# Ordering the next group's weight sums behind the running group's addition on VectorE, in a two-layer hybrid trunk

## The chip, the cores and the metric

The kernel runs on one core of a Trainium2 chip. The metric is the time of one execution on the device in microseconds (us). TensorE multiplies matrices, VectorE and ScalarE do elementwise work, GpSimd (POOL) does a little elementwise work and issues accumulating DMAs, and SyncE (SP) issues the loads. Each engine works through its own list of instructions in order; engines wait for each other on semaphores. Matrix products land in eight banks of PSUM, everything else lies in SBUF.

## The reference, cut to what matters

Two layers over 512 tokens of width 1024, all in float32. Each layer is a mixer with a residual and then a gated feed-forward part with a residual. The change touches only the feed-forward part:

```python
def gated_conv_ffn(x, w_gate, w_up, conv_w, conv_b, w_down):
    g = jnp.einsum('bsd,df->bsf', x, w_gate)        # 1024 -> 2816
    g = causal_dwconv3(g, conv_w) + conv_b          # width 3 along the tokens
    up = jnp.einsum('bsd,df->bsf', x, w_up)         # 1024 -> 2816
    return jnp.einsum('bsf,fd->bsd', jax.nn.silu(g) * up, w_down)

hn = rms_norm(h, norm_ffn[layer])
h = h + gated_conv_ffn(hn, w_ffn_gate[layer], w_ffn_up[layer], conv_ffn[layer],
                       b_conv_ffn[layer], w_ffn_down[layer])
```

The mixers (a short gated convolution and causal pooling in the first layer, chunked spatial gating in the second) and the final norm are not touched.

## The kernel before, in words

**Precision.** Every float32 operand is split into a high part `hi`, rounded to the matmul's input format, and the rest `lo = x - hi`. A product is three matmuls into one bank: hi by hi, hi by lo, lo by hi. ScalarE writes `hi` (names `whi_...`, `a_hi`), VectorE writes `lo` (`wlo_...`, `a_lo`). For some weights (`summed`, L116) ScalarE writes `-x` into `lo`, a DMA from GpSimd adds `x`'s raw value to it (L121), and ScalarE writes `hi` (L122).

**The groups of the feed-forward part.** The hidden width of 2816 is 22 tiles of 128 columns, taken two at a time; a group `f` is the tiles f and f+1. `PARTS` (L475) sets the order: groups 0, 2, then 4, then the pairs (6, 8), (10, 12), (14, 16) and (18, 20). After each entry of `PARTS` the tiles finished so far are multiplied with their rows of the down weight. So inside a pair the second group follows the first with no down product between. Groups from 4 on are computed by `both` (L636).

**One group in `both`.** The gate matrix ("g") and the up matrix ("u") of the group, 1024 rows by 256 columns each, and the tokens are seen as 2 by 2 blocks, and each matrix is multiplied in seven products instead of eight, by sums of blocks (a scheme of Strassen's kind). A product is 12 matmuls of 128 by 256. `ffn_weights` loads four raw tiles of 512 KB (gate and up, upper and lower half of the rows) into four buffers with the tag "raw"; the next group's loads take the same buffers. From the raw tiles come:

- L646-648: block a11 of both matrices, split by `halves` (`whi_a11` and `wlo_a11`, `whi_a` and `wlo_a` in the profile); it feeds product 1.
- L653, L654: VectorE sums `s12` (lower right blocks added, then one block taken off), split into `whi_s12` and `wlo_s12`; they feed products 5 and 6.
- L659, L660: VectorE differences `s34`, split likewise; they feed products 7 and 3.
- L661: the lower half of the raw rows, split by `summed`; it feeds products 2 and 4.

L694 multiplies in the order gate 1, up 1, gate 5, gate 6, up 5, up 6, gate 2, gate 7, up 2, up 7, gate 4, gate 3, up 4, up 3. Products 1, 6, 7 and 4 of a matrix add up in one bank ("a"), 5 and 3 in a second ("e"), and 2 has a third ("b"). After each product `after` (L680) takes out what is needed: ScalarE copies (L682) products 1, 6, 7 and the gate's 4 from bank "a" into `rows3` (gate, name `rows`) or `kept` (up) before the next product of that bank adds to it. VectorE adds product 2 (bank "b") and product 3 (bank "e") onto such a copy (L687). When product 7 has been copied, VectorE adds product 5 from bank "e" onto the copy (L692); only then may product 3 overwrite bank "e".

Behind the gate's products come the width-3 convolution (`conv`: ScalarE L505, VectorE twice L507 per tile), the SiLU on ScalarE (`s`, L513), the products with the up matrix (L703, L704, L707) and the split of the result (`act`: `a_hi` L247, `a_lo` L249).

**Who sets the order.** The instructions are recorded in the order of the program text, and a list scheduler orders each engine's list by priorities and by its own estimate of times, so that instructions of the next group can stand ahead of the running group's. Each engine then runs its list strictly in that order. `tc.keep_in_program_order` and `tc.add_manual_dep` can bind the order.

The lines that stand in question:

```python
nc.vector.tensor_tensor(s12[:, 0], r0[:, :, P:], r1[:, :, P:], ALU.add)          # L653
nc.vector.tensor_tensor(s34[:, 0], r0[:, :, :P], r0[:, :, P:], ALU.subtract)     # L659
nc.vector.tensor_tensor(d, pending[key, 5], d, ALU.add)                          # L692
```

Of the kernel before, what the change touches and what calls it, by code (L numbers as in the profile page):

```python
# [12 lines left out]
ALU = mybir.AluOpType  # L13
PSUM = bass.MemoryType.PSUM

P = 128
# [14 lines left out]
def tile_trunk(ctx: ExitStack, tc: tile.TileContext, x, norm_mix, norm_ffn, final_norm,  # L31
# [3 lines left out]
    nc = tc.nc  # L35
# [37 lines left out]
            ("bf", rows_of(b_conv_ffn[1]), NF)])  # L73

    inorder = tc.keep_in_program_order

    eps = small[:, 1:2]
    nc.gpsimd.memset(eps, EPS)
# [37 lines left out]
    def summed(raw, a, b, name):  # L116

        hi = wp.tile([P, a, b], F32R, tag="whi", bufs=6, name=f"whi_{name}")
        lo = wp.tile([P, a, b], F32R, tag="wlo", bufs=6, name=f"wlo_{name}")
        nc.scalar.activation(lo, raw, AF.Copy, scale=-1.0)  # L120
        nc.gpsimd.dma_start(lo, raw, accum_op=ALU.add)  # L121
        nc.scalar.activation(hi, raw, AF.Copy)  # L122
        return hi, lo
# [42 lines left out]
    class Norm:  # L166


        def __init__(self, name, gain, apart=False):
            self.name, self.gain, self.n, self.apart = name, gain, 0, apart  # L170
            self.ssq = tp.tile([P, S], F32, tag="ssq", bufs=1, name=f"ssq_{name}")
# [97 lines left out]
    def padded_tile():  # L269
        turn[0] += 1  # L270
        return padded[turn[0] % NPADDED]
# [209 lines left out]
    def ffn_weights(layer, f, order):  # L481
        cs = slice(f * P, (f + 2) * P)
        return {(key, half): fetch(
            (w_ffn_gate if key == "g" else w_ffn_up)[layer][half * 512 : (half + 1) * 512, cs]
            .rearrange("(k p) c -> p k c", p=P), 4, 256, f"{key}{layer}_{f}_{half}")
            for key, half in order}

    class Ffn:
# [8 lines left out]
        def __init__(self, layer, prm, norm, ap, sums):  # L497
            self.layer, self.prm, self.ap, self.acts = layer, prm, ap, {}
            self.norm, self.sums = norm, sums
            self.t23, self.t41 = {}, {}  # L500

        def conv(self, t, ft):
            ap, prm, n = self.ap, self.prm, f"{self.layer}_{ft}"
            c = ap.tile([P, S], F32, tag="c", bufs=2, name=f"c{n}")
            nc.scalar.activation(c, t[:, 0:S], AF.Copy, scale=prm("cf", ft))  # L505
            for i in (1, 2):
                nc.vector.scalar_tensor_tensor(c, t[:, i : S + i], prm("cf", i * NF + ft), c,  # L507
                                               op0=ALU.mult, op1=ALU.add)
            return c
# [126 lines left out]
        def both(self, f):  # L636

            layer, ap, n = self.layer, self.ap, f"{self.layer}_{f}"
            raws = ffn_weights(layer, f, [(key, half) for half in range(2) for key in "gu"])
            stat = {}  # L640

            def put(key, product, hi_lo, i):
                stat[key, product] = hi_lo[0][:, i], hi_lo[1][:, i]

            w = self.unit(f"a11_{n}")
            for i, key in enumerate("gu"):  # L646
                self.halves(w[0][:, i], w[1][:, i], raws[key, 0][0][:, :, :P])
                put(key, 1, w, i)
            for key in "gu":
                r0, r1 = raws[key, 0][0], raws[key, 1][0]  # L650
                s12, s34 = (ap.tile([P, 2, 4, P], F32, tag="sum", bufs=3, name=f"{x}{key}_{n}")
                            for x in ("s12", "s34"))
                nc.vector.tensor_tensor(s12[:, 0], r0[:, :, P:], r1[:, :, P:], ALU.add)  # L653
                nc.vector.tensor_tensor(s12[:, 1], s12[:, 0], r0[:, :, :P], ALU.subtract)  # L654
                w = self.unit(f"s12{key}_{n}")
                self.halves(*w, s12)
                put(key, 5, w, 0)
                put(key, 6, w, 1)
                nc.vector.tensor_tensor(s34[:, 0], r0[:, :, :P], r0[:, :, P:], ALU.subtract)  # L659
                nc.vector.tensor_tensor(s34[:, 1], r1[:, :, :P], s12[:, 1], ALU.subtract)  # L660
                hi, lo = summed(*raws[key, 1])  # L661
                for i, product in enumerate((2, 4)):
                    c = slice(i * P, (i + 1) * P)
                    stat[key, product] = hi[:, :, c], lo[:, :, c]
                w = self.unit(f"s34{key}_{n}")
                self.halves(*w, s34)
                put(key, 7, w, 0)
                put(key, 3, w, 1)

            banks = {"g": {}, "u": {}}  # L670
            kept = ap.tile([P, 3, HALF], F32, tag="kept", bufs=1, name=f"kept{n}")
            pads = [padded_tile() for _ in range(2)]
            lo, hi = slice(2, 2 + HALF), slice(2 + HALF, 2 + S)
            dst = {("g", 1): pads[0][:, lo], ("g", 6): pads[0][:, hi], ("g", 7): pads[1][:, hi],
                   ("g", 4): pads[1][:, lo]}
            dst.update({("u", product): kept[:, i, :] for i, product in enumerate((1, 6, 7))})
            onto = {2: 1, 5: 7, 3: 6}
            s, pending = {}, {}

            def after(key, product, ps):  # L680
                if (key, product) in dst:
                    nc.scalar.copy(dst[key, product], ps)  # L682
                elif product == 5 and (key, 7) not in pending:
                    pending[key, 5] = ps
                elif product in onto:
                    d = dst[key, onto[product]]
                    nc.vector.tensor_tensor(d, ps, d, ALU.add)  # L687
                if (key, product) == ("u", 4):
                    pending["u", 4] = ps
                if product == 7:  # L690
                    d = dst[key, 7]
                    nc.vector.tensor_tensor(d, pending[key, 5], d, ALU.add)  # L692

            for key, product in (("g", 1), ("u", 1), ("g", 5), ("g", 6), ("u", 5), ("u", 6),  # L694
                                 ("g", 2), ("g", 7), ("u", 2), ("u", 7), ("g", 4), ("g", 3),
                                 ("u", 4), ("u", 3)):
                after(key, product, self.multiply(banks[key], f"{key}{n}", product,
                                                  stat[key, product]))
                if (key, product) == ("g", 4):
                    s[1] = self.silu(self.conv(pads[1], f + 1), f + 1)  # L700
                elif (key, product) == ("g", 3):
                    s[0] = self.silu(self.conv(pads[0], f), f)
            nc.vector.tensor_tensor(s[1][:, HALF:], kept[:, 2, :], s[1][:, HALF:], ALU.mult)  # L703
            nc.vector.tensor_tensor(s[1][:, :HALF], pending["u", 4], s[1][:, :HALF], ALU.mult)  # L704
            self.act(f + 1, s[1])
            s0 = s[0].rearrange("p (a b) -> p a b", a=2)
            nc.vector.tensor_tensor(s0, kept[:, :2, :], s0, ALU.mult)  # L707
            self.act(f, s[0])
# [284 lines left out]
```

## Time and profile before

| | |
|---|---|
| three runs | 1005.27, 1007.35, 1007.23 us; median 1007.23 |
| profiled execution | 1007.18 us, its span 1005.5 us |
| granted TensorE clock | 0.996 |
| TensorE busy | 988.0 us, 98% of the span, 5835 matmuls |
| VectorE busy | 699.3 us, 70%, 1057 instructions |
| ScalarE busy | 521.9 us, 52% |
| GpSimd busy | 100.8 us, 10% |
| HBM read, written | 98.42 MB, 2.10 MB |

How to read it: the profile is of one execution. A row of the timeline has a start and a duration in us, the engine, the line of the kernel, the operation, the tile written and the tiles read with buffer numbers left out, the shape, and in square brackets how long the engine was idle just before, with the engine, tile and line that released it. Rows that follow each other alike are merged (x4). Tile names carry the group: `g_6e` is bank "e" of the gate matrix in group 6; whether a row belongs to layer 0 or 1 is told by its time: the feed-forward part of layer 0 ends before 500 us and that of layer 1 begins after 620 us. `s12g`, `s34u` and the like carry the matrix, and `whi`/`wlo` in front of them are their high and low parts. A time is in the clock of the span.

### The profile page before, as it was taken

What the parts mean: (1) busy time and instruction counts of PE and PEld (TensorE: products, weight loads), DVE (VectorE), ACT (ScalarE), POOL (GpSimd) and SP (SyncE); (2) the same over time, 40 slices, a digit from 0 to 9 for tenths busy, and PEclk for the clock granted to TensorE, in tenths of its full rate; (3) what the DMA queues carried; (4) which work ended last, traced back from release to release, by engine and by line L of the source; (5) the groups of instructions that cost most, each with busy time, mean ns of one, the idle gap of its engine ahead of it and who ended that gap; (6) DMA issues with size and microseconds to landing.
All of it is one profiled execution on the core that took longest, in us unless ns stands there. A gap on an engine that the chain in (4) does not pass through costs nothing.

```text
span 1005.5 us, 14738 instructions
## 1 busy us (share of the span) xinstructions
PE 988.0 (98%) x5835; PEld 875.6 (87%) x5835; DVE 699.3 (70%) x1057; ACT 521.9 (52%) x775; POOL 100.8 (10%) x117
## 2 busy tenths in 40 slices
PE   8999999999999999999999999999999999999997
PEld 6788888898999989899888888888999899898895
DVE  5877457968776786867933545399667867687577
ACT  5622345744653746537655443675446366363563
POOL 2132020300000000000300001211000010000100
PEclk9999999999999999999999999999999999999999
DMA  6522224454454545545433222445446465454532
GB/s 222 191 96 92 85 84 126 105 150 123 129 147 129 162 113 132 147 115 167 134 118 105 74 93 91 98 97 132 129 105 156 117 142 152 102 152 125 123 109 83
DMA packets 81905, 124.53 MB, mean 124 GB/s; under 512 B 4293, under 2 KB 53677, under 8 KB 81837
## 3 DMA queue, kind: packets, MB, share of 16 engines
q1 hardware_dynamic: 73580, 98.96, 31.1%
q0 software_dynamic: 6912, 23.07, 12.5%
q10 hardware_dynamic: 1344, 1.58, 0.5%
q8 instruction: 45, 0.74, 0.3%
q14 instruction: 24, 0.19, 0.1%
HBM read 98.42 MB, written 2.10 MB: 100 GB/s over the span
## 4 chain that ended last, share of the span: by engine, by line
PE 81%; issue 7%; DMA 5%; DVE 5%; ACT 2%; POOL 0%; SPq 0%; ACTq 0%; DVEq 0%; POOLq 0%
PE gu L133 3%; PE gu L134 3%; PE gu L135 3%; PE d L133 3%; PE d L134 3%; PE d L135 3%; PE dn L133 2%; PE dn L135 2%; PE dn L134 2%; DMA raw_g<-in_w_ffn_gate_dram 2%; PE u L135 1%; PE oo L135 1%; PE u L134 1%; PE oo L133 1%; PE u L133 1%
## 5 line engine op out<-in xcount | busy, mean ns | idle before, releaser
L507 DVE SCALAR_TENSOR_TENSOR c<-rows,prm,c 128x512 f32<-128x512 f32 x88 | 67.7, 792 | 4.4 <-ACT c L505 4.1
L134 PE MATMUL d<-a_lo,whi_d 128*128 128x512 f32 x176 | 68.6, 390 | 0.0
L133 PE MATMUL dn<-whi_dn,a_hi 128*128 128x512 f32 x176 | 68.6, 390 | 0.0
L134 PE MATMUL dn<-wlo_dn,a_hi 128*128 128x512 f32 x176 | 68.6, 390 | 0.0
L135 PE MATMUL d<-a_hi,wlo_d 128*128 128x512 f32 x176 | 68.5, 389 | 0.0
L135 PE MATMUL dn<-whi_dn,a_lo 128*128 128x512 f32 x176 | 67.3, 390 | 0.0
L133 PE MATMUL d<-a_hi,whi_d 128*128 128x512 f32 x176 | 66.9, 390 | 0.0
L121 POOL DMA_DIRECT2D wlo_g<-raw_g x22 | 19.1, 868 | 382.1 <-ACT wlo_g L120 315.9
L922 DVE TENSOR_TENSOR y<-dn,y 128x512 f32<-128x512 f32 x48 | 32.3, 686 | 22.8 <-PE dn L135 22.3
L120 ACT ACTIVATE wlo_g<-raw_g 128x1024 fp32r<-128x1024 f32 x22 | 23.2, 1055 | 42.4 <-PE dn L134 42.4
L129 DVE TENSOR_TENSOR wlo_u<-raw_u,whi_u 128x1024 fp32r<-128x1024 f32 x16 | 19.6, 1224 | 34.2 <-ACT whi_u L128 34.1
L513 ACT ACTIVATE s<-c,prm 128x512 f32<-128x512 f32 x44 | 30.8, 716 | 21.5 <-DVE c L507 21.5
L633 ACT ACTIVATE whi_s12u<-s12u 128x1024 fp32r<-128x1024 f32 x18 | 18.9, 1049 | 43.2 <-PE d L134 33.8
L633 ACT ACTIVATE whi_s12g<-s12g 128x1024 fp32r<-128x1024 f32 x18 | 19.1, 1061 | 41.7 <-DVE s12g L654 36.1
L129 DVE TENSOR_TENSOR wlo_dn<-raw_dn,whi_dn 128x1024 fp32r<-128x1024 f32 x22 | 26.8, 1221 | 19.0 <-ACT whi_dn L128 19.0
L135 PEld LDWEIGHTS dn<-whi_dn,a_lo 128*128 128x128 f32 x176 | 33.0, 188 | 7.5 <-DVE a_lo L249 0.2
L134 PEld LDWEIGHTS d<-a_lo,whi_d 128*128 128x128 f32 x176 | 33.0, 188 | 7.3 <-DVE a_lo L249 0.2
L133 PEld LDWEIGHTS dn<-whi_dn,a_hi 128*128 128x128 f32 x176 | 33.0, 188 | 7.1 <-ACT a_hi L247 0.2
L129 DVE TENSOR_TENSOR wlo_d<-raw_d,whi_d 128x1024 fp32r<-128x1024 f32 x22 | 26.8, 1221 | 17.9 <-ACT whi_d L128 17.9
L133 PEld LDWEIGHTS d<-a_hi,whi_d 128*128 128x128 f32 x176 | 32.8, 188 | 7.1
L292 DVE TENSOR_TENSOR h<-d,h 128x512 f32<-128x512 f32 x48 | 32.5, 685 | 9.3 <-PE d L135 9.3
L135 PEld LDWEIGHTS d<-a_hi,wlo_d 128*128 128x128 f32 x176 | 33.0, 188 | 6.8
(1201 smaller groups left out, 3423.4 us busy)
## 6 DMA issues: line engine op xcount, KB each, us to landing
raw_g<-in_w_ffn_gate_dram SPq DMA_DIRECT2D x36, 512.0 KB, 4.1
raw_u<-in_w_ffn_up_dram SPq DMA_DIRECT2D x36, 512.0 KB, 4.5
wlo_g<-raw_g POOLq DMA_DIRECT2D x22, 512.0 KB, 4.6
raw_d<-in_w_ffn_down_dram SPq DMA_DIRECT2D x22, 512.0 KB, 3.6
raw_dn<-in_w_ffn_down_dram SPq DMA_DIRECT2D x22, 512.0 KB, 3.5
wlo_u<-raw_u POOLq DMA_DIRECT2D x18, 512.0 KB, 4.6
raw_oe<-in_w_out_even_dram SPq DMA_DIRECT2D x8, 512.0 KB, 3.6
raw_g<-in_w_ffn_gate_dram SPq DMA_DIRECT2D x16, 256.0 KB, 2.8
```

What stands on the lines that cost most here:

```text
L120: nc.scalar.activation(lo, raw, AF.Copy, scale=-1.0)
L121: nc.gpsimd.dma_start(lo, raw, accum_op=ALU.add)
L129: nc.vector.tensor_tensor(lo, raw, hi.bitcast(F32), ALU.subtract)
L133: nc.tensor.matmul(ps, lhs[0], rhs[0], start=start, stop=False)
L134: nc.tensor.matmul(ps, lhs[0], rhs[1], start=False, stop=False)
L135: nc.tensor.matmul(ps, lhs[1], rhs[0], start=False, stop=stop)
L292: nc.vector.tensor_tensor(h[k], ps, h[k], ALU.add)
L507: nc.vector.scalar_tensor_tensor(c, t[:, i : S + i], prm("cf", i * NF + ft), c, op0=ALU.mult, op1=ALU.add)
L513: nc.scalar.activation(s, c, AF.Silu, bias=self.prm("bf", ft))
L633: nc.scalar.activation(hi, src, AF.Copy)
L922: nc.vector.tensor_tensor(dst, ps, dst, ALU.add)
```

## The change: an order between two instructions of VectorE

`Ffn` remembers, for each of the two matrices, the last recorded addition L692. In the next group, the first sum of `s12` (L653) and the first difference of `s34` (L659) of the same matrix get a dependency on it that is only an order on the same engine, with no semaphore. Nothing is computed otherwise, and no buffer changes. In the first group of `both` there is no earlier addition, and no dependency. The dependency also holds where a down product lies between two groups.

```diff
+    def behind(ins, first):
+
+        if first is not None:
+            tc.add_manual_dep(ins.ins, first.ins.name, mybir.DependencyInfo(
+                mybir.DependencyClass.NoSync, mybir.DependencyReason.DATA), reason="order")
...
             self.t23, self.t41 = {}, {}
+            self.added = {"g": None, "u": None}
...
-                nc.vector.tensor_tensor(s12[:, 0], r0[:, :, P:], r1[:, :, P:], ALU.add)
+                behind(nc.vector.tensor_tensor(s12[:, 0], r0[:, :, P:], r1[:, :, P:], ALU.add),
+                       self.added[key])
                 nc.vector.tensor_tensor(s12[:, 1], s12[:, 0], r0[:, :, :P], ALU.subtract)
...
-                nc.vector.tensor_tensor(s34[:, 0], r0[:, :, :P], r0[:, :, P:], ALU.subtract)
+                behind(nc.vector.tensor_tensor(s34[:, 0], r0[:, :, :P], r0[:, :, P:],
+                                               ALU.subtract), self.added[key])
                 nc.vector.tensor_tensor(s34[:, 1], r1[:, :, :P], s12[:, 1], ALU.subtract)
...
                 if product == 7:
                     d = dst[key, 7]
-                    nc.vector.tensor_tensor(d, pending[key, 5], d, ALU.add)
+                    self.added[key] = nc.vector.tensor_tensor(d, pending[key, 5], d, ALU.add)
```

In the changed kernel every line from `behind` on has a number that is 6 to 9 higher: L692 is L701 there.

## The prediction

> **What bounds the kernel now.** I read the page first, then the waits of TensorE in its timeline, and from each of them back along VectorE and ScalarE. From the page:
>
> ```profile
> span 1005.5 us, 14738 instructions
> ...
> PE 81%; issue 7%; DMA 5%; DVE 5%; ACT 2%; POOL 0%; SPq 0%; ACTq 0%; DVEq 0%; POOLq 0%
> ```
>
> TensorE carries the chain, so only what makes TensorE wait can be won. Its timeline, a start and a duration in us per row, has these waits in the stage that the change touches:
>
> ```profile
> 451.47 0.39 PE L624 MATMUL g_18e<-hgh,whi_s34g 128*128 128x256 f32 x1 [0.59 <-DVE rows L692]
> ...
> 759.91 0.38 PE L624 MATMUL g_6e<-hgh,whi_s34g 128*128 128x256 f32 x1 [1.07 <-DVE rows L692]
> 760.13 0.28 PE L624 MATMUL g_6e<-hgl,whi_s34g 128*128 128x256 f32 x1
> 760.25 0.28 PE L624 MATMUL g_6e<-hgh,wlo_s34g 128*128 128x256 f32 x1
> ...
> 820.61 0.50 PE L624 MATMUL u_10a<-t,whi_s34u 128*128 128x256 f32 x2 [1.02 <-ACT kept L682]
> ...
> 823.99 0.38 PE L624 MATMUL g_10e<-hgh,whi_s34g 128*128 128x256 f32 x1 [0.25 <-DVE rows L692]
> ...
> 951.41 0.39 PE L624 MATMUL g_18e<-hgh,whi_s34g 128*128 128x256 f32 x1 [2.44 <-DVE rows L692]
> ```
>
> Four of the five are the first matmul of the gate's product 3 (the bank "e" of the running group), held by the addition L692 on VectorE, which must read product 5 out of that bank first. The fifth, 820.61, is the up matrix's product 7, held by ScalarE's copy L682 of product 6. Each costs more than its idle figure: a record of 0.28 stands for a step of 0.12 (760.13 to 760.25), so 0.16 of the wait lies under the record before, and the step behind the wait is 0.22 (759.91 to 760.13), 0.10 too long. So delay = idle + 0.26: 0.85, 1.33, 1.28, 0.51, 2.70, in all 6.67 us. The VectorE rows ahead of two of them show why:
>
> ```profile
> 758.23 0.69 DVE L653 TENSOR_TENSOR s12u<-raw_u,raw_u 128x512 f32<-128x512 f32 x1 [1.66 <-DMA raw_u<-in_w_ffn_up_dram]
> 758.84 0.68 DVE L659 TENSOR_TENSOR s34u<-raw_u 128x512 f32<-128x512 f32 x1
> 759.44 0.41 DVE L692 TENSOR_TENSOR rows<-g_6e,rows 128x256 f32<-128x256 f32 x1
> ...
> 949.19 0.69 DVE L653 TENSOR_TENSOR s12u<-raw_u,raw_u 128x512 f32<-128x512 f32 x1 [4.20 <-DMA raw_u<-in_w_ffn_up_dram]
> 949.80 1.22 DVE L634 TENSOR_TENSOR wlo_s12g<-s12g,whi_s12g 128x1024 fp32r<-128x1024 f32 x1
> 950.93 0.42 DVE L692 TENSOR_TENSOR rows<-g_18e,rows 128x256 f32<-128x256 f32 x1
> ```
>
> At 758.23 VectorE had sat 1.66 us, at 949.19 it had sat 4.20 us, waiting for the load of the next group's up weights (L653), with L692 of the running group queued behind. L692 starts 1.21 and 1.74 us after the landing and TensorE 0.06 us after its end (759.85 to 759.91). ScalarE has the same queueing at 820.61 (and the running group's copy of product 7 at 882.26 in a quiet case):
>
> ```profile
> 819.24 1.06 ACT L633 ACTIVATE whi_s12g<-s12g 128x1024 fp32r<-128x1024 f32 x1 [4.86 <-DVE s12g L654]
> 820.20 0.35 ACT L682 COPY kept<-u_10a 128x256 f32<-128x256 f32 x1
> ...
> 882.26 0.37 ACT L682 COPY rows<-g_14a 128x256 f32<-128x256 f32 x1 [0.39 <-PE g_14a L624]
> ```
>
> The copy `kept` at 820.20 needed only TensorE, but stood behind `whi_s12g`, which had waited 4.86 us for the next group's sums.
>
> **The change part by part.** No instruction is added or removed, and no semaphore: the order is between instructions of one engine. Set against each other, the two programs differ at eight places, the four handovers 6 to 8, 10 to 12, 14 to 16 and 18 to 20 of each layer. There L687 and L692 of the gate now stand ahead of the next group's gate sums, and both gate and up additions ahead of its up sums. The scheduler follows up elsewhere: ScalarE's `kept` copies move ahead of `whi_s12g`; s34u's last sum (L660) with its `whi` and `wlo` goes behind `wlo_s12u`; `wlo_s34g` and the two `a_lo` go ahead of `wlo_s12u`; TensorE takes the up product 5's second part 10 matmuls later, behind the gate's product 6.
>
> *What goes.* L692 now waits only for the copy of product 7, which ends at 882.63 in the handover 14 to 16, 3.8 us before product 3 starts there:
>
> ```profile
> 886.40 0.38 PE L624 MATMUL g_14e<-hgh,whi_s34g 128*128 128x256 f32 x1
> ```
>
> So the four L692 waits end; and the one on `kept` too, because that copy no longer has `whi_s12g` ahead of it. That is 6.67 us, plus the 0.10 that the row at 886.40 lost to a wait of 0.02: 6.77 us.
>
> *What comes.* Eight additions and sums now run later, so I walk VectorE's new order through 14 to 16. Steps between starts come from rows: 0.60 for 128x512 (758.84 to 759.44), and from these
>
> ```profile
> 888.13 0.42 DVE L687 TENSOR_TENSOR rows<-g_14e,rows 128x256 f32<-128x256 f32 x1
> 889.38 2.74 DVE L507 SCALAR_TENSOR_TENSOR c<-rows,prm,c 128x512 f32<-128x512 f32 x4 [0.82 <-ACT c L505]
> 892.04 0.42 DVE L687 TENSOR_TENSOR kept<-u_14e,kept 128x256 f32<-128x256 f32 x1
> 892.37 1.22 DVE L634 TENSOR_TENSOR wlo_s34g<-s34g,whi_s34g 128x1024 fp32r<-128x1024 f32 x1
> 893.50 0.42 DVE L703 TENSOR_TENSOR s<-kept,s 128x256 f32<-128x256 f32 x1
> ```
>
> 0.33 for 128x256 (892.04 to 892.37), 1.13 for 128x1024 (892.37 to 893.50), 0.66 for one L507 (four from 889.38 to 892.04). Product 3 now ends 0.12 earlier, so L687 starts at 888.01. Behind it two up sums: 888.34, 888.94. The four L507 run from 889.54 instead of 889.38, `kept` 892.20, L703 892.53, L704, L707 893.19, `wlo_s34g` 893.79, two `a_lo` 894.92 and 895.52, `wlo_s12u` 896.12 to 897.34. ScalarE beside it:
>
> ```profile
> 891.76 1.32 ACT L513 ACTIVATE s<-c,prm 128x512 f32<-128x512 f32 x2
> 892.99 1.04 ACT L122 ACTIVATE whi_u<-raw_u 128x1024 fp32r<-128x1024 f32 x1
> 893.93 1.04 ACT L633 ACTIVATE whi_s34u<-s34u 128x1024 fp32r<-128x1024 f32 x1
> 894.88 1.14 ACT L247 ACTIVATE a_hi<-s 128x512 fp32r<-128x512 f32 x2
> 895.92 1.05 ACT L120 ACTIVATE wlo_u<-raw_u 128x1024 fp32r<-128x1024 f32 x1
> 896.87 0.35 ACT L682 COPY rows<-g_16a 128x256 f32<-128x256 f32 x1
> ...
> 898.93 1.06 ACT L128 ACTIVATE whi_dn<-raw_dn 128x1024 fp32r<-128x1024 f32 x1 [1.44 <-PE g_16a L624]
> ```
>
> L703 needs `s`, whose first half ends about 892.5: in time. With `whi_s34u` gone from 893.93 the two `a_hi` take 893.93 to 894.97, and the copy `rows` of the next gate product 1 runs 894.97 to 895.32.
> TensorE, from 886.38 in steps of 1.44 per product: the next group's product 1 of gate 890.70 and up 892.14, gate 5 at 893.58; then, in the new order, 2 matmuls of up 5 and 1 of gate 2; gate 6 at 895.38; 2 of up 6 and 4 of gate 2; the rest of up 5 at 897.54. Gate 6 needs `rows`: 895.32 + 0.06 = 895.38, nothing to spare. The rest of up 5 needs `wlo_s12u`: 897.34 + 0.06 = 897.40, 0.14 to spare. A wait of any size costs the 0.10 behind it, so I take 0.10 for each of the seven handovers like this one, 0.70 us; the ends are 0 (`rows` just in time, as 886.40 nearly was) and 0.30 (`rows` 0.20 late).
>
> *Late loads.* Up sums now stand behind L692 of up, about 0.95 us after product 4 starts, so a landing up to then costs nothing. In 6 to 8 of layer 1 product 3 was due at 759.91 - 1.23 = 758.68, product 4 at 757.24, the sum could start at 758.2, the load was in at 758.23. In 18 to 20 of layer 1 product 3 was due at 951.41 - 2.60 = 948.81, its load was in at 949.19, 0.87 past that point. There the walk from 949.19 is: `wlo_s12g` 949.80, L687 950.93, three up sums, L507 from 953.06, `kept` 955.72, L703, L704, `wlo_s34g` 956.71, L707, one `a_lo`, `wlo_s12u` 959.04 to 960.26. TensorE's order there puts all of gate 2 ahead of the rest of up 5, due at 959.37. So 0.95 + 0.10 = 1.05 us of the 2.70 stays. It goes to 0 if the load lands 0.9 earlier, which can be: the load of `fin` (512 KB, ScalarE's queue) now is issued behind `whi_s12g` rather than beside this load. In the other handovers the sum followed straight on other work or came early; I take their loads as in time.
>
> *What is covered.* L660 of s34u, its `whi` and `wlo` end about 900.3; the product that reads them comes at 903.8. The first down-weight load must wait for the later gate sums, until about 885.3; the page gives its flight:
>
> ```profile
> raw_dn<-in_w_ffn_down_dram SPq DMA_DIRECT2D x22, 512.0 KB, 3.5
> ```
>
> so it lands near 889, and its reader `whi_dn` starts at 898.93. If this cover of 10 us went, each handover would pay the rest. The later loads of SP's queue wait for POOL's accumulating DMAs, as before. `wlo_u` goes out about 0.3 earlier; POOL's order is the same.
>
> *Sum.* Against the profiled execution's 1007.18 us (the median of the runs shown is 1007.23, so nothing is corrected): 1007.18 - 6.77 + 1.05 + 0.70 = 1002.2 us.
>
> **The rivals.**
> 1. All waits go: `rows` is in time everywhere and the load lands early. 1007.18 - 6.77 = 1000.4. For it: 886.40 waited 0.02 only. Against it: nothing to spare seven times over.
> 2. The tight place gives more: 0.35 in each of seven handovers, where ScalarE or VectorE runs 0.25 late. 1007.18 - 6.77 + 1.05 + 2.45 = 1003.9.
> 3. The stall moves: VectorE or `rows` comes some 0.7 late at each of eight places, and what L692 gave is paid at gate 6 and up 5 again; about 1007. The rows speak against it: ScalarE's chain from 888 to 893 stays as it was, since `s` is set by ScalarE's own order.
> 4. Slower: VectorE starts an instruction only when the one before has ended. Then the walk goes by durations, not by steps: from 888.01 0.42, 2 x 0.68, 4 x 0.75, 3 x 0.42, 0.68, 1.22, 2 x 0.68, 1.22 make 898.53, 1.05 past its point, with the 0.10 behind it 1.15 at seven places and 1.05 + 0.85 in 18 to 20: 1007.18 - 6.77 + 8.05 + 1.90 = 1010.4. It decides from 0.7 us per handover on. Against it: 758.84 starts 0.08 before the end of 758.23's record, and all rows above step so. The Trainium skill's page VectorE: DVE Perf Modes (The DRAIN you can't avoid) states that the next op does not start until the pipe has emptied after the one before. By that rule the time is this rival's; the trace disagrees with it in 0.61 steps under 0.69 records.
> 5. The change does nothing: excluded, the order of eight handovers changes.
>
> **How the numbers follow.** The forecast 0.60; rival 1 0.12; rival 2 0.12; rival 3 0.08; rival 4 0.08. A measurement of this kernel tells about 0.2%, 2 us, from no change. Faster by more: the first three, 0.84; same 0.08; slower 0.08. The range leaves out rivals 3 and 4: from 1000.2, just under rival 1, to 1005.0, rival 2 with the runs' own scatter (1005.27 to 1007.35 before).
>
> **What would show it.** In the changed profile product 3 (g_6e, g_10e, g_14e, g_18e) waits for no L692 (there L701), u_10a not for `kept`; L653 of the next group starts behind L692. Right at the tight place: short waits of g_8a, g_12a, g_16a and g_20a for `rows`, or of u_8e and its like for `wlo_s12u`; a wait of about 1 us at u_20e of layer 1. The prediction is wrong if these exceed 0.4 us each, or if loads of up weights land over 1 us later than here.

## The result, and the profile after

| | before | after |
|---|---|---|
| median | 1007.13 us (6 runs, 1004.08 to 1007.48) | 1000.98 us (6 runs, 1000.02 to 1002.09) |
| profiled execution | 1007.18 us | 1000.02 us |
| TensorE, VectorE, ScalarE busy | 988.0, 699.3, 521.9 us | 986.5, 699.9, 522.7 us |

The ratio is 0.9948, with a 95% interval of 0.9933 to 0.9962: 5.2 us less (3.8 to 6.7); the medians differ by 6.2. The forecast was 1002.2 us in a range of 1000.2 to 1005.0, faster with 0.84. The page of the changed kernel:

```profile
span 998.3 us, 14727 instructions
...
PE 92%; DVE 4%; DMA 2%; ACT 1%; issue 0%; SPq 0%; POOL 0%; DVEq 0%; ACTq 0%; POOLq 0%
```

The engines do the same work: TensorE, VectorE, ScalarE and GpSimd have 5835, 1057, 775 and 117 instructions in both pages, and the busy times move by 1.5 us at most, so what was won is waiting. The shares of the chain that ends last do not measure it: TensorE has 92% where it had 81%, and "issue" fell from 7% to 0%, which is some 70 us, where 5 us were won. Without the waits the chain takes another way back through the program; e9 below, still faster than before, has TensorE at 77%. TensorE's timeline of the changed kernel, at the places that the prediction named:

```profile
765.20 0.28 PE L631 MATMUL g_8b<-hgh,whi_g 128*128 128x256 f32 x1
765.32 0.51 PE L631 MATMUL g_8a<-t,whi_s12g 128*128 128x256 f32 x2
765.66 0.29 PE L631 MATMUL g_8a<-t,wlo_s12g 128*128 128x256 f32 x1
...
881.12 0.28 PE L631 MATMUL g_14e<-hgh,whi_s34g 128*128 128x256 f32 x1
...
954.59 0.39 PE L631 MATMUL u_20e<-t,wlo_s12u 128*128 128x256 f32 x1 [0.33 <-DVE wlo_s12u L641]
```

Product 3 of the gate (`g_14e`, 881.12) has no bracket, and neither have `g_6e`, `g_10e`, `g_18e` and `u_10a`: the five waits are gone in both layers. One wait is new, 0.33 idle at `u_20e`. At 765.32 two matmuls run before 765.66: 0.34 for two steps of 0.12, so one step was 0.10 too long, at the place where `rows` was to have nothing to spare. The same long step stands at `g_8a`, `g_12a`, `g_16a` and `g_20a` of both layers, eight in all. VectorE in the handover 18 to 20 of layer 1:

```profile
939.83 0.42 DVE L701 TENSOR_TENSOR rows<-g_18e,rows 128x256 f32<-128x256 f32 x1 [1.42 <-ACT rows L691]
940.17 0.68 DVE L660 TENSOR_TENSOR s12g<-raw_g,raw_g 128x512 f32<-128x512 f32 x1
940.77 0.69 DVE L667 TENSOR_TENSOR s34g<-raw_g 128x512 f32<-128x512 f32 x1
...
943.03 0.42 DVE L701 TENSOR_TENSOR kept<-u_18e,kept 128x256 f32<-128x256 f32 x1
943.37 0.68 DVE L660 TENSOR_TENSOR s12u<-raw_u,raw_u 128x512 f32<-128x512 f32 x1
...
952.72 0.68 DVE L255 TENSOR_TENSOR a_lo<-s,a_hi 128x512 fp32r<-128x512 f32 x1
953.32 1.22 DVE L641 TENSOR_TENSOR wlo_s12u<-s12u,whi_s12u 128x1024 fp32r<-128x1024 f32 x1
```

The addition (L701, L692 before) now comes first and has waited only for the copy of product 7; the first up sum at 943.37 follows the up addition with no idle time, where before it had held VectorE for 4.20 us.

Not all of the 7.2 us between the two profiled spans is the change. To tell it apart I measure from the start of each feed-forward part's first matmul to the start of its last: from the first `gu` to the last `d` in layer 0, the second `gu` to the program's last matmul in layer 1. The rows of before and, behind them, of after:

```profile
149.51 0.39 PE L133 MATMUL gu<-hgh,whi_g 128*128 128x512 f32 x1
...
497.79 0.39 PE L135 MATMUL d<-a_hi,wlo_d 128*128 128x512 f32 x1
...
640.79 0.48 PE L133 MATMUL gu<-hgh,whi_g 128*128 128x512 f32 x1
...
997.65 0.39 PE L135 MATMUL dn<-whi_dn,a_lo 128*128 128x512 f32 x1
```

```profile
147.92 0.39 PE L139 MATMUL gu<-hgh,whi_g 128*128 128x512 f32 x1
...
495.43 0.39 PE L141 MATMUL d<-a_hi,wlo_d 128*128 128x512 f32 x1
...
638.44 0.48 PE L139 MATMUL gu<-hgh,whi_g 128*128 128x512 f32 x1
...
990.52 0.39 PE L141 MATMUL dn<-whi_dn,a_lo 128*128 128x512 f32 x1
```

Layer 0 takes 348.28 before and 347.51 after, layer 1 takes 356.86 and 352.08: 0.77 + 4.78 = 5.55 us won in the two parts. The other 1.59 us were already there at the first `gu` (149.51 to 147.92), in work that the change doesn't touch. "Stage gain" below is this sum against before's 705.14 us; it needs no median, and a second profile of the changed kernel (e11) gives 5.43. Before's stage is from one profile; e3, which leaves layer 0 as it was, has 348.61 there where before has 348.28, so differences of 0.3 us say little.

### The profile page after: what moved, and what is told of

It is laid out like the page before. It is cut to its first block, busy times and chain, and to the rows that moved or that the text cites. A ratio compares the mean times of both kernels' runs of the same rounds, so it can differ in the third digit from the quotient of the medians.

```text
span 998.3 us, 14727 instructions
## 1 busy us (share of the span) xinstructions
PE 986.5 (99%) x5835; PEld 874.5 (88%) x5835; DVE 699.9 (70%) x1057; ACT 522.7 (52%) x775; POOL 100.6 (10%) x117
## 3 DMA queue, kind: packets, MB, share of 16 engines
q10 hardware_dynamic: 1344, 1.58, 0.5%
## 4 chain that ended last, share of the span: by engine, by line
PE 92%; DVE 4%; DMA 2%; ACT 1%; issue 0%; SPq 0%; POOL 0%; DVEq 0%; ACTq 0%; POOLq 0%
PE d L139 4%; PE d L140 4%; PE d L141 4%; PE dn L139 4%; PE dn L140 3%; PE dn L141 3%; PE gu L139 3%; PE gu L141 3%; PE gu L140 3%; PE u L141 1%; PE oo L141 1%; PE oo L139 1%; PE u L140 1%; PE u L139 1%; PE oe L140 1%; PE oe L139 1%
## 5 line engine op out<-in xcount | busy, mean ns | idle before, releaser
L641 DVE TENSOR_TENSOR wlo_s34u<-s34u,whi_s34u 128x1024 fp32r<-128x1024 f32 x18 | 22.1, 1226 | 26.1 <-ACT whi_s34u L640 26.1
L140 PEld LDWEIGHTS dn<-wlo_dn,a_hi 128*128 128x128 f32 x176 | 33.1, 188 | 6.5
```

The lines of the kernel that those rows point to most:

```text
L140: nc.tensor.matmul(ps, lhs[0], rhs[1], start=False, stop=False)
L641: nc.vector.tensor_tensor(lo, src, hi.bitcast(F32), ALU.subtract)
```

## The experiments

The ratios are against runs of before beside each group: its median was 1007.32 us beside e1 to e4, 1006.6 beside e5 to e8, 1006.56 beside e9 and e10, and 1006.77 beside e11 and e12. The stage gain is of one profile each.

| run | what it is | median, us | ratio (95%) | stage gain, us |
|---|---|---|---|---|
| e1 | only the up sums bound | 1002.99 | 0.9960 (0.9948 to 0.9973) | 4.37 |
| e2 | e1 and ScalarE's copy first | 1001.93 | 0.9958 (0.9943 to 0.9973) | 3.40 |
| e3 | the change in layer 1 only | 1002.03 | 0.9956 (0.9941 to 0.9970) | 4.35 |
| e4 | no dependency, early up load | 999.40 | 0.9931 (0.9917 to 0.9945) | 7.07 |
| e5 | the change on e4 | 1000.1 | 0.9940 (0.9927 to 0.9953) | 6.11 |
| e6 | only ScalarE's copy first | 1005.5 | 0.9989 (0.9976 to 1.0001) | -1.54 |
| e7 | first up sum behind the gate's addition | 1002.9 | 0.9963 (0.9949 to 0.9976) | 3.53 |
| e8 | only the gate sums bound | 1003.14 | 0.9964 (0.9950 to 0.9979) | 3.51 |
| e9 | the change, up load 1.8 us later | 1003.63 | 0.9970 (0.9959 to 0.9982) | 3.00 |
| e10 | e5, up load delayed likewise | 999.99 | 0.9938 (0.9920 to 0.9955) | 6.02 |
| e11 | the change again | 1000.78 | 0.9942 (0.9928 to 0.9956) | 5.43 |
| e12 | e4 again, beside e11 | 999.24 | 0.9926 (0.9913 to 0.9939) | 7.08 |

**e1, only the up sums.** TensorE, ScalarE and the queues keep the lists of before; only VectorE's order differs.

```diff
-                    self.added[key] = nc.vector.tensor_tensor(d, pending[key, 5], d, ALU.add)
+                    last = nc.vector.tensor_tensor(d, pending[key, 5], d, ALU.add)
+                    if key == "u":
+                        self.added[key] = last
```

> Only the up matrix's sums are bound behind the up matrix's addition; the gate's sums stay where they were, and the lists of TensorE, ScalarE, GpSimd and SyncE are those of the kernel before, instruction for instruction; on VectorE the additions L692 of both matrices now stand ahead of the up sums. Theory A (TensorE's wait for L692 behind the late up load is what the change removes): the waits of 18e in layer 0 and of 6e, 10e, 14e and 18e in layer 1, 5.49 us with what follows each, go; the wait of u_10a for the copy `kept`, 1.28 us, stays; the 0.10 at gate 6 in eight handovers does not come. 1007.1 - 5.5 = 1001.6 us, ratio 0.9945. Theory B (the gain comes from what the scheduler moved on ScalarE and TensorE): at most 1 us of gain, 1006 or more, ratio 0.999.

Measured 1002.99 us, a stage gain of 4.37: theory A, 1.4 us short of it. The waits for the addition are gone, so it is the up sums behind a late load that made them. Two waits remain in its TensorE timeline:

```profile
819.13 0.51 PE L631 MATMUL u_10a<-t,whi_s34u 128*128 128x256 f32 x2 [0.94 <-ACT kept L691]
...
956.78 0.39 PE L631 MATMUL g_20b<-hgh,wlo_g 128*128 128x256 f32 x1 [0.54 <-DMA wlo_g<-raw_g]
```

The first is the old wait for `kept`. The second is new: TensorE, freed of its 2.70 us at `g_18e`, comes to the gate's product 2 of group 20 before the accumulating DMA of `wlo_g` has landed, and gives 0.80 back.

**e2, with ScalarE's copy.** e1, and `whi_s12g` behind the copy `kept` of product 6 (cut):

```diff
-            nc.scalar.activation(hi, src, AF.Copy)
+            behind(nc.scalar.activation(hi, src, AF.Copy), first)
...
-                self.halves(*w, s12)
+                self.halves(*w, s12, self.copied if key == "g" else None)
...
-                    nc.scalar.copy(dst[key, product], ps)
+                    copied = nc.scalar.copy(dst[key, product], ps)
+                    if (key, product) == ("u", 6):
+                        self.copied = copied
```

> As the run with the up sums alone, and ScalarE's `whi_s12g` is bound behind the running group's copy `kept` of up product 6; TensorE's list is that of the kernel before. Theory A: u_10a no longer waits for `kept` either, but product 3 of group 10 is then due 1.28 us earlier, at 822.30 in the old clock, and L692, behind the sums of the gate, whose load lands at 817.2, ends at 822.74; so some 0.6 us of it comes back there. 1007.1 - 6.2 = 1000.9 us, ratio 0.994, and no wait of 0.10 at gate 6. Theory B: 1005 or more.

The wait for `kept` is gone, but the stage gain fell to 3.40: TensorE now waits for `wlo_g` at `g_20b` with 1.58 idle, and twice for `wlo_u` at `u_16b`. The 0.6 us that theory A expected back at `g_10e` did not come; the accumulating DMAs took more than that. The median, 1001.93, does not show this loss against e1; the intervals overlap. So by the profile the copy's 1.28 us was not won.

**e3, layer 1 only.** The recording of the addition gets a condition; the fence is cut to it.

```diff
+                    if layer == 1:
+                        self.added[key] = last
```

> The order is bound in layer 1 alone. Theory A: layer 1 lost 5.9 us to the waits before and loses about 1.0 after (0.49 + 0.10 at u_20e and four times 0.10 at gate 6), so 4.9 us of the change's gain is there and 0.45 us in layer 0 (0.85 less four times 0.10): 1007.1 - 4.9 = 1002.2 us, ratio 0.995; in layer 0 the wait of g_18e is back. Theory C (the gain is spread, or is scatter of the start of the program): ratio between 0.997 and 1.

1002.03 us. Layer 1 gains 4.68 as in the full change (4.78). In layer 0 the old wait stays, 0.92 idle here where it was 0.59, with the same program there: a wait for a load moves by 0.3 us from one execution to another. The two layers' gains add up: 4.68 here and 0.77 in layer 0 of the full change make 5.45 of its 5.55.

**e4, the early load.** No dependency is added, and the list scheduler orders the engines anew. In the first group of each pair the up matrix's lower half is split by ScalarE and VectorE (`parts`) rather than by the accumulating DMA:

```diff
-                hi, lo = summed(*raws[key, 1])
+                split = parts if key == "u" and f in (6, 10, 14, 18) else summed
+                hi, lo = split(*raws[key, 1])
```

> The order of the kernel before, with the up sums still ahead of L692; instead the cause of the late up load is taken away: in groups 6, 10, 14 and 18 the low part of up's lower half is a subtraction on VectorE (1.2 us each) instead of the accumulating DMA, so that the raw buffer is free some 4 to 7 us earlier for the next group's up load. Theory A: VectorE no longer sits for that load ahead of L692, the waits of g_6e, g_14e and g_18e go or fall under 0.3 us, that of u_10a for `kept` behind the gate's sums stays: about 1002.5 us, ratio 0.9955. Theory D (it is the order itself, VectorE's queue being full, and not the late load): the waits stay, 1007 or more.

999.40 us, less than either theory gave and less than the changed kernel. Loads (SP) and accumulating DMA (POOL) of before, and then the loads of e4, in the handover 18 to 20 of layer 1:

```profile
936.82 0.86 POOL L121 DMA_DIRECT2D wlo_u<-raw_u  x1 [3.87 <-DMA wlo_g<-raw_g]
...
936.69 0.37 SPq L110 DMA_DIRECT2D raw_g<-in_w_ffn_gate_dram  x1
944.27 0.37 SPq L110 DMA_DIRECT2D raw_u<-in_w_ffn_up_dram  x1
```

```profile
931.29 0.37 SPq L110 DMA_DIRECT2D raw_g<-in_w_ffn_gate_dram  x1
931.75 0.99 SPq L110 DMA_DIRECT2D raw_u<-in_w_ffn_up_dram  x1
...
943.08 0.28 PE L624 MATMUL g_18e<-hgh,whi_s34g 128*128 128x256 f32 x1
```

Before, the up load is issued 7.45 us after the accumulating DMA of the group before, which reads the same raw buffer and itself had waited 3.87 us for the gate's; that is 7.58 us after the gate's load. In e4 it is issued 0.46 us after it. The late load comes from this DMA. With it gone no wait of TensorE is left in either feed-forward part (943.08 has no bracket), although the gate's addition (L693 here) still stands behind the up sums on VectorE. The wait for `kept`, which theory A kept, went by another way: in layer 1 the scheduler put ScalarE's copy ahead of `whi_s12g`, as it did in the changed kernel. Rows of e4, VectorE in the handover 18 to 20 and then ScalarE in 10 to 12, both of layer 1:

```profile
939.01 0.69 DVE L653 TENSOR_TENSOR s12u<-raw_u,raw_u 128x512 f32<-128x512 f32 x1
...
942.29 0.42 DVE L693 TENSOR_TENSOR rows<-g_18e,rows 128x256 f32<-128x256 f32 x1
```

```profile
811.69 0.37 ACT L683 COPY kept<-u_10a 128x256 f32<-128x256 f32 x1 [1.53 <-PE u_10a L624]
814.39 1.06 ACT L633 ACTIVATE whi_s12g<-s12g 128x1024 fp32r<-128x1024 f32 x1 [2.33 <-DVE s12g L654]
```

So e4 shows the source of the waits for L692; it does not show that of the wait for `kept`. Also gone are four long first steps that before and after share, at `g_6a`, `g_10a`, `g_14a` and `g_18a` of layer 1, 0.17 us each; that is how it gains more than the 6.77 us of the prediction's list, though it has some ten steps of its own that are 0.05 too long.

**e5, the order on the early load.** The changed kernel with e4's edit.

> The change on top of e4: the up weights' lower half is split without the accumulating DMA in the groups 6, 10, 14 and 18, and the sums stand behind the additions as in the changed kernel. Theory L (late up loads are the whole cause of the waits for L692, and the new order only moves VectorE out of their way): e4 has no wait left in the stage, so the order has nothing to win; it brings its eight long steps of 0.10 at the next group's gate product 6, and the wait at u_20e is gone because the load is early: 999.4 + 0.8 = 1000.2 us, ratio 0.993 to 0.994, slower than e4 in the profile by 0.8. Theory O (the order is worth something by itself, beside late loads): below 999.0. Theory X (the eight splits of about 1.1 us that go to VectorE make its new, tight order late at gate 6 or up 5): waits of 0.5 to 1.2 in most handovers, 1004 to 1008 us.

1000.1 us, stage gain 6.11: theory L. The new order has nothing to win once the load is early, and costs 0.96 us: the eight long steps of 0.10, another of 0.10 in group 20 and the 0.59 at `u_20e`, less some ten steps in e4, 0.05 too long, that it does not have. That wait I had not expected here:

```profile
932.10 1.43 SPq L116 DMA_DIRECT2D raw_u<-in_w_ffn_up_dram  x1
...
954.53 0.39 PE L631 MATMUL u_20e<-t,wlo_s12u 128*128 128x256 f32 x1 [0.33 <-DVE wlo_s12u L641]
```

In the changed kernel it is as long, with the load issued 6.8 us later:

```profile
938.90 0.37 SPq L116 DMA_DIRECT2D raw_u<-in_w_ffn_up_dram  x1
```

So it does not come from the load.

**e6, ScalarE's copy alone.** Of e2 only the three edits shown there, with VectorE's sums as before.

> Of the change only what ScalarE does: whi_s12g stands behind the copy kept of up product 6; VectorE keeps the sums ahead of the additions. Theory A (each wait is worth its own price): the wait of u_10a goes, 1.28 us, 1006.0 us. Theory B (the waits are in a row behind one late load): TensorE comes to g_10e 1.28 us earlier and waits there for L692 that much longer, 0.51 becomes about 1.8; 1007.3 us, no change, ratio 0.999 to 1.001.

1005.5 us, ratio up to 1.0001: no gain that can be told. TensorE no longer waits at `u_10a` and waits longer for the addition right behind it:

```profile
821.88 0.38 PE L631 MATMUL g_10e<-hgh,whi_s34g 128*128 128x256 f32 x1 [1.11 <-DVE rows L701]
```

1.11 idle instead of 0.25, a delay of 1.37 where it was 0.51: theory B, if short of its 1.8. The accumulating DMA of `wlo_u` takes another 0.70 at `u_16b`. Its stage loss of 1.54 is that of one disturbance of the clock, told below.

**e7, the first up sum behind the gate's addition.** At the first sum of `s12`:

```diff
-                       self.added[key])
+                       self.added["g"] if key == "u" else None)
```

with the dependency of `s34` left out.

> Only the first up sum is bound, and behind the gate's addition L692; no other sum is bound. TensorE and ScalarE keep the order of before. Theory A (what stalls is the gate's addition behind a late up load): the four L692 waits and the 0.10 at g_14e go, 5.49 us; the wait of u_10a for kept (1.28) stays and, as in e1, the wait for wlo_g at g_20b comes (0.80): about 4.5 us gained, 1002.8 us, ratio 0.9955. Theory B (the up addition, now behind the late up load, stops up product 3 in turn): u_6e and u_18e wait for L700 by 0.3 to 1.3 us: 1004 us or more.

1002.9 us as theory A said, but by other waits. The four L692 waits and that for `kept` went; 0.20 and 0.26 came at `u_6e` and `u_18e`, as theory B said and smaller, and the accumulating DMA took its share:

```profile
946.55 0.86 POOL L127 DMA_DIRECT2D wlo_g<-raw_g  x1 [13.76 <-ACT wlo_g L126]
...
955.36 0.38 PE L631 MATMUL g_20b<-hgh,wlo_g 128*128 128x256 f32 x1 [1.82 <-DMA wlo_g<-raw_g]
```

The wait for `kept` went although ScalarE's copy still stands behind `whi_s12g` here. What differs is the gate's load that these sums wait for; VectorE in 10 to 12 of layer 1, in before and then in e7:

```profile
817.23 0.69 DVE L653 TENSOR_TENSOR s12g<-raw_g,raw_g 128x512 f32<-128x512 f32 x1 [4.99 <-DMA raw_g<-in_w_ffn_gate_dram]
```

```profile
811.86 0.69 DVE L660 TENSOR_TENSOR s12g<-raw_g,raw_g 128x512 f32<-128x512 f32 x1 [2.77 <-DMA raw_g<-in_w_ffn_gate_dram]
```

From its issue to this row that load took 6.22 us in before (811.01 to 817.23), 6.32 in e1 and 6.87 in e6, but 4.52 in e7 (807.34 to 811.86). So the 1.28 us at `u_10a` needs the order and a slow load together; why the load is slow in three profiles and not in this one is open.

**e8, only the gate sums.** As e1 with `"g"`; TensorE and ScalarE get the order of the changed kernel.

> Only the gate sums are bound, behind the gate's addition; the up sums are free and stand ahead of the up addition. TensorE and ScalarE get the order of the changed kernel. Theory A (the gate's addition is what had to be freed, and the up sums come behind it of themselves): as the changed kernel, with its long steps of 0.10 and about 0.6 at u_20e: 1001.0 us, ratio 0.994. Theory B (both orders are needed): a wait for an addition stays or comes at up product 3 of layer 1, 0.5 us or more in one or two handovers: 1002 to 1003 us.

1003.14 us, stage gain 3.51: theory B's time, not its place. No addition holds TensorE; it waits for `wlo_u` and at `u_20e`:

```profile
900.59 0.39 PE L631 MATMUL u_16b<-hgh,wlo_u 128*128 128x256 f32 x1 [0.41 <-DMA wlo_u<-raw_u]
...
958.66 0.39 PE L631 MATMUL u_20e<-t,wlo_s12u 128*128 128x256 f32 x1 [0.88 <-DVE wlo_s12u L641]
```

Each half of the change alone wins, by the profiles, 3.5 to 4.4 of its 5.5 us and then meets other waits, the accumulating DMA in both. In the whole change ScalarE writes `wlo_g` ahead of `whi_g` in 18 to 20 of layer 1, so its DMA is issued 1.83 us after product 3 starts (945.37 to 943.54) and not 2.65 (e7: 946.55 to 943.90), with the reader due 9.1 us after that start: 7.3 us of room instead of 6.5. In e1 and e7 it was 7.2 and 8.8 us from the issue to the reader, so this room is enough for the one and would not be for the other.

**e9 and e10, a later load.** A small load into the same buffer goes ahead of the up load of the second group of each pair (`LATE` holds the names of these loads), in the changed kernel (e9) and in e5 (e10):

```diff
+        if name in LATE:
+            nc.sync.dma_start(raw[:, :1, :64], src[:, :1, :64])
         nc.sync.dma_start(raw, src)
```

> The changed kernel, with the load of the next group's up weights (lower half) made late in the eight handovers, by a small load into the same buffer that must land first: estimated at 1.5 to 2.5 us, from the 2.8 us of a load of 256 KB. In the changed kernel the first up sum starts 8.7 us after the issue of that load in layer 0 (7.6 in 18 to 20) and 4.5 to 5.0 us after it in layer 1, and such a load takes about 4.1 us: so 3.5 to 4.6 us to spare in layer 0 and 0.4 to 0.9 in layer 1. Theory L (the order moves VectorE out of the way of a late load, as far as that room goes): layer 0 shows no wait, each handover of layer 1 pays 0.6 to 2.1 us, in all 2.5 to 8; about 1006 us, the gain gone. Theory F (behind the additions the load has room everywhere): 1001 to 1002 us.

> The same delay of the same loads in e5, where they are issued some 7 us earlier and the first up sum follows 11 to 13 us after the issue. Theory L: 4 us or more to spare everywhere, so nothing is paid: as e5, 1000.1 us, ratio 0.9935. Theory D (the delay costs by itself, through the queue of loads behind it): as e9, 1003 us or more.

e9's loads and VectorE:

```profile
940.46 0.34 SPq L118 DMA_DIRECT2D raw_u<-in_w_ffn_up_dram  x1
942.29 0.37 SPq L119 DMA_DIRECT2D raw_u<-in_w_ffn_up_dram  x1
...
946.07 0.69 DVE L663 TENSOR_TENSOR s12u<-raw_u,raw_u 128x512 f32<-128x512 f32 x1 [1.36 <-DMA raw_u<-in_w_ffn_up_dram]
```

The delay is 1.83 us. Layer 0 pays nothing (347.54 against 347.51). In layer 1 VectorE waits again and the part takes 354.60 instead of 352.08: 2.52 us more, the median 2.7 above the changed kernel's. e10, where the same small load delays the up load by 3.5 to 3.9 us in layer 1, pays nothing (999.99 against 1000.1). Theory L in both; the price lies at the low end, because in 6 to 8 and 10 to 12 VectorE took nearly all of the delay up before TensorE (0.29 and nothing there).

**e11 and e12, the two best beside each other.**

> The changed kernel once more, beside e12 on the same chip. Both theories: as before, 1001.0 us, ratio 0.995.

> The kernel of e4 once more, beside e11. Theory E (the early load alone beats the changed order, by the 1.5 us that the two profiles' stages differ): 999.4 us, ratio 0.993, 1 to 2 us under e11. Theory S (the difference of the two medians was scatter of other executions): within 0.5 us of e11.

1000.78 and 999.24 us on one chip, runs from 1000.12 to 1002.02 and from 998.43 to 1000.03: theory E. The stage gains repeat to 0.12. By this the kernel of e4 is the faster of the two, 1.5 us under the changed one.

## Why the prediction was right, and where it was not

**What goes** was right: all four waits for L692 and the one for `kept` went. That the up sums behind a late load were the cause of the four is shown from two sides, by e1 (move the sums) and e4 (move the load). The price of the `kept` wait counts only together with the rest: alone (e6) 0.86 of its 1.28 us came back in the very next wait. It also needs a slow gate load: in e7 it went with the copy where it was.

**What comes** was right in place and size per handover: 0.10 each at gate 6, from `rows` just in time. The rows in which ScalarE's copy ends 0.06 before the matmul at 765.32:

```profile
763.87 1.14 ACT L253 ACTIVATE a_hi<-s 128x512 fp32r<-128x512 f32 x2
764.91 0.35 ACT L691 COPY rows<-g_8a 128x256 f32<-128x256 f32 x1
```

764.91 + 0.35 = 765.26, and TensorE at 765.32, 0.06 behind it, as the walk had it. There are eight such places, not seven, and one more of 0.10 in group 20: 0.90 against 0.70.

**Late loads** failed. The step kept 1.05 us at `u_20e` for a load landing too late, and said that an earlier landing would bring it to 0. The wait came, at 0.49 plus 0.10, but e5 has it unchanged with the load 6.8 us earlier. VectorE's order there puts one `a_lo` ahead of `wlo_s12u`, which ends at 954.54 in the changed kernel (953.32 + 1.22) where TensorE would have come at 954.10; the load hides under that. The prediction's own walk gives this when it starts from product 3 instead of the load: the addition of product 3 (L687 before, L696 now) starts 1.64 after product 3 (943.54 to 945.18), 8.11 more of the walk, 1.22 and 0.06 make 11.03, and TensorE comes 10.56 after product 3: 0.47 to pay with any load. So the step that failed is the 0.95 put down to the load, and with it the claim that an earlier landing brings it to 0. That the load took less time than before is true as well: the first up sum started 4.47 us after the issue (938.90) without a wait, against 4.92.

The terms as measured: 6.77 - 0.90 - 0.59 = 5.28, against a stage gain of 5.55 and 5.43; the remaining 0.2 to 0.3 are not traced. The prediction had 5.02: 0.20 too little for the long steps and 0.46 too much for `u_20e`, two errors that partly cancel, which is luck. Its 5.02 lies inside the measured interval of 3.8 to 6.7. The rest of its miss against the median, 1002.2 to 1000.98, lies mostly outside the stage: it was reckoned from a profiled execution whose first `gu` came at 149.51, while in the thirteen other profiles of this study it came at 147.87 to 148.99. Whether that start was chance is not settled.

**The rivals.** Rival 1 (all goes, 1000.4) is nearer to the median than the forecast, but not by its mechanism, as the long steps and `u_20e` are there. Rivals 2 and 3: no handover pays 0.35 at the tight place. Rival 4: the steps of 0.60 under records of 0.68 stand in the changed kernel too (940.17 to 940.77), and no handover is late by its 1.15. The Trainium skill's page VectorE: DVE Perf Modes (The DRAIN you can't avoid) states that the next operation does not start until the pipe is empty, which the prediction read as the end of the record before; that reading would have made the change slower, and the trace disagrees with it here as before. The same section adds that a next operation that is not held starts earlier, so the rows speak against that reading and not against the page.

**What I passed over.** Two things. The prediction weighed the up load's lateness as given; its source, the accumulating DMA of the group before, is the better lever (e4). And it named no cover for the accumulating DMAs of the next group beyond "as before": `wlo_g` had been hidden by the very wait that goes, and in the whole change it was just covered, with ScalarE's order having moved it 0.82 us forward (1.83 against 2.65). The prediction did not foresee this, so it was luck. e1, e2 and e7 paid 0.8 to 2.1 us there. By the same kind of room, e9 shows the changed kernel to stand near an edge: 1.8 us of lateness take back 2.5 of its 5.5 us.

## What to carry to other kernels

When an engine stands in order behind a late load, moving its other work ahead of the wait wins what was queued there; but look first for what made the load late, since removing that (here a DMA that held the buffer) can win as much without a tighter order; here it won 1.5 us more. Price every wait that goes together with the next ones behind it: TensorE arrives earlier at all of them, and a transfer that was covered by the old wait can become the new one. Test a reordering with the load made later by a known amount; that shows how much of the gain is room and how much is luck.

## What the runs showed of the hardware that was not expected

- A first step that is 0.10 us too long stands on TensorE also where it hardly waited: at 765.32 it started 0.12 us after the matmul before, as without a wait, and the two matmuls there took 0.34 us instead of 0.24. Its size goes with how early the copy `rows` ends: in the changed kernel it ends 0.04 to 0.06 before the matmul at all eight places, in e4 0.10 to 0.12 before, with a step 0.04 to 0.06 too long, and in before's group 20 of layer 1 0.24 before, with no long step.
- The accumulating DMA of 512 KB has a median of 4.8 us from issue to landing on the changed kernel's page (`wlo_g`, x22), but in the handover 18 to 20 of layer 1, next to other loads, 7.2 us (e1) and 8.8 us (e7) passed from its issue to the release of its reader; in e4 a reader 6.5 us after the issue (945.73 to 952.20) did not wait.
- A load of 32 KB ahead of another into the same buffer holds it for 1.83 us in e9 (940.46 to 942.29), and for 3.92 us in e10 (931.94 to 935.86), 0.57 us after the issue of the gate's load (931.37).
- In e6, behind a wait of 2.66 us at `g_18e`, the granted clock was halved for 3.4 us (951.47 to 954.88). The windows of that kernel (columns: window, its length, busy time and count of PE, PEld, DVE, ACT and POOL, granted clock, DMA share, GB/s):

```profile
948.00:951.50 3.50, 1.08 (x9) 1.09 (x10) 3.30 (x6) 2.67 (x4) 0.86 (x1) 0.99 0.00 0
951.50:955.00 3.50, 3.50 (x20) 3.50 (x19) 3.37 (x7) 1.76 (x3) 0.00 (x0) 0.52 1.01 180
```

  Steps of 0.21 to 0.22 instead of 0.12 cost it about 1.5 us. Before's wait of 2.44 us at the same place had no such effect (granted clock 1.00 in the same two windows), and it was seen in this one profile only; what sets it off stays open.
